# The first layer's SSM tables, rotations and rotary embedding moved from GpSimd to VectorE

## The chip, the cores and the metric

One core of a Trainium2 chip runs the kernel. The metric is the device time in microseconds, the median of several runs of the same program. The profile is of one further execution. Below, PE is the matrix engine, DVE is VectorE, ACT is ScalarE, POOL is GpSimd, and SP is the engine that issues most of the DMAs.

## The reference

Two layers of a hybrid backbone work on 512 latent tokens and 256 context tokens of width 1024. A layer norms and modulates its input (adaLN), projects it once, splits the projection into five parts, mixes tokens in three ways, projects back, and ends with a SwiGLU FFN. Cut to what the change touches:

```python
h  = modulate(rmsnorm(x, g_pre_mix), sh1, sc1) @ w_in          # the same for the context
u, f, q, k, v = jnp.split(h, splits, axis=-1)                  # 384, 256, 384, 384, 384 channels

lam_bar = jnp.exp(lam * dt)                                    # 24 groups, 64 complex states each, 2 directions
b_bar = ((lam_bar - 1) / lam)[..., None] * bmat
hc = ssm_scan(lam_bar, einsum('gph,blgh->blgp', b_bar, ucg), None, rev)
h  = ssm_scan(lam_bar, einsum('gph,blgh->blgp', b_bar, ug), h0, rev)
y  = y + einsum('ghp,blgp->blgh', cmat, h).real
z  = gelu(y);  y_ssm = z * sigmoid(z @ w_glu)

q, k = axial_rope(q, row, col), axial_rope(k, row, col)        # x1*cos - x2*sin, x2*cos + x1*sin
y_na = na_latent(q, k, v, kc, vc, na_rpb)                      # 2-D neighbourhood attention plus context
```

All inputs are 32-bit floats. The first layer also puts the context through everything; the last one leaves out the context's output.

## The kernel before

Activations lie with channels on the partitions. For each large product the left and the right side are split into a high part that PE can read (fp32r) and a low rest, and three products are added: high by high, high by low, low by high. A split is an ACT copy to the high part and a subtraction on DVE or POOL (`split`, `sub`, L579, L561). Weights come by DMA into a ring of two raw tiles and are split the same way (`wload`).

`build` (L1262) begins with the modulation vectors (`mod`), the norms of six token tiles, the scalars and powers of the SSM's eigenvalues (`scalars`, `powers`), and `make_h`: it transposes each normed tile on PE, scales and shifts it (L555, DVE), and splits it. The subtraction of the split goes to DVE for even k and to POOL for odd k.

The SSM works on chunks of 8 tokens, 96 chunk columns with the context at both ends. Twelve steps k = 2u + d go over six groups of four heads (u) and two directions (d). For each k three things are made and used:

- The tables (`prep_dir`, L430): the B table bm by three DVE operations (L447 to L449), transposed on PE (L464); the C table cl by three POOL operations of 128x576 (L452 to L456); a kernel of short lags kp on PE (L480) from cl and a padded slice b0 of bm; and the phases (`phase`, L395): index times turn, reduced to a fraction by two DVE operations, then Abs and two Sin on ACT. In the first layer they are made on the spot, one k ahead (AHEAD0); for the second they are made during the first layer's FFN, kept in DRAM and loaded again.
- The scan (`ssm_scan`, L711): PE makes the drive (L721), DVE rotates it by the phases (L725 to L728; two of the operations cross the halves of the partitions) and scans it (L731), and POOL rotates it back (L734 to L744).
- The output (`ssm_out`, L747): PE adds the states and the short lags (L756, L758); for odd k a gelu follows on ACT and DVE.

`w_in` projects eleven chunks of 128 channels: u first, then k and q in turn, then f. Chunks of q and k go through `rope` (L686): an ACT copy, a shuffle on DVE, a product on POOL (L695), a product and a sum on DVE, and splits that are stored to DRAM.

The SSM's steps are woven with the chunks of `w_in` (L1321), then come `w_v`, the Fourier mixer, the GLU and attention. The order on each engine is the framework's: a scheduler with a timeline model takes the instructions in the program's order of priority and fixes each engine's queue. In a queue the engine works in order, and an instruction that waits holds up those behind it.

Of the kernel before, what the change touches and what calls it, by code (L numbers as in the profile page):

```python
# [8 lines left out]
F32 = mybir.dt.float32  # L9
F32R = mybir.dt.float32r  # L10
I32 = mybir.dt.int32
AF = mybir.ActivationFunctionType
ALU = mybir.AluOpType
# [8 lines left out]
NH, HD = 6, 64  # L22
# [12 lines left out]
class Builder:  # L35
    def __init__(self, tc, ctx, ap):
        self.tc, self.nc, self.ap = tc, tc.nc, ap
        pool = lambda name, bufs, **k: ctx.enter_context(tc.tile_pool(name=name, bufs=bufs, **k))
        self.ring_raw = pool("ring_raw", 2)
        self.ring_hi = pool("ring_hi", 4)  # L40
        self.ring_lo = pool("ring_lo", 4)
        self.tab_p = pool("tab", 3)
        self.x_p = pool("xp", 3)
        self.g_p = pool("gp", 2)
        self.u_p = pool("up", 1)
        self.s_p = pool("sp", 24)
        self.q_p = pool("qp", 12)
        self.c_p = pool("cp", 22)
        self.z_p = pool("zp", 2)
        self.sm_p = pool("sm", 18)  # L50
        self.ss_p = pool("ss", 12)
        self.am_p = pool("am", 24)
        self.b0_p = pool("b0p", 2)
        self.keep = pool("keep", 1)
        self.ps_p = {t: pool("ps_" + t, n, space=PSUM) for t, n in (("m", 3), ("a", 2), ("t", 2), ("o", 1))}
        self.dr_p = pool("dr", 1, space=DRAM)
# [39 lines left out]
    def consts(self):  # L96
        nc = self.nc
        self.cols = self.k("cols", [128, 8])
        nc.sync.dma_start(self.cols, self.ap["cols"])
        self.ident = self.k("ident", [128, 128])  # L100
        self.nidx = self.k("nidx", [128, 96])
        self.eye16 = self.k("eye16", [128, 16])
        self.junk = self.k("junk", [128, 512], mybir.dt.bfloat16)
        self.zero = self.k("zero", [1, 128], mybir.dt.bfloat16)
        nc.vector.memset(self.zero, 0.0)
        self.sgn, self.nsgn, self.sgn2pi, self.halfpi = (self.cols[:, i:i + 1] for i in range(4))
        self.mhalf = self.cols[:, 4:5]
        self.qd = [self.dram(f"qd{l}", [NH * HD, 2, NT]) for l in range(DEPTH)]
        self.kd = [self.dram(f"kd{l}", [NH * HD, 2, NT]) for l in range(DEPTH)]
        self.ud = [self.dram(f"ud{l}", [G, HC, 8, 128]) for l in range(DEPTH)]  # L110
        self.zd = [self.dram(f"zd{l}", [G, HC, 8, 96]) for l in range(DEPTH)]
        self.tabd = [self.dram(f"tabd{l}", [NU, 2, 128, 1792]) for l in range(DEPTH)]
        self.wd = [self.dram(f"wd{l}", [NU, 128, 240]) for l in range(DEPTH)]
        self.gd = [self.dram(f"gd{l}", [4, DM]) for l in range(DEPTH)]
        self.rbd = [self.dram(f"rbd{l}", [NH, 16, 8, 384]) for l in range(DEPTH)]
        self.xd = [self.dram(f"xd{l}", [6, 128, DM]) for l in range(3)]
        self.turn = [self.k(f"turn{l}", [128, 48]) for l in range(DEPTH)]
        self.rho = [self.k(f"rho{l}", [128, 48]) for l in range(DEPTH)]
        self.mcol = [[self.k(f"mc{l}{a}", [128, 2, 16]) for a in range(3)] for l in range(DEPTH)]
        self.gcol = [self.k(f"gcol{l}", [128, 2, 8]) for l in range(DEPTH)]  # L120
        self.amod = [[self.k(f"am{l}{i}", [128, 2, 8]) for i in range(2)] for l in range(DEPTH)]
        self.dcol = [self.k(f"dcol{l}", [128, NU]) for l in range(DEPTH)]

    def consts_load(self):
        nc = self.nc
        nc.sync.dma_start(self.ident, self.ap["ident"])
        nc.sync.dma_start(self.nidx, self.ap["nidx"])
        nc.sync.dma_start(self.eye16, self.ap["eye16"])
        for l in range(DEPTH):
            nc.sync.dma_start(self.gcol[l], self.ap["gpre"][l])  # L130
            nc.sync.dma_start(self.dcol[l], self.ap["ssm_d"][l])
# [263 lines left out]
    def phase(self, l, u, d, dst):  # L395

        o = (u * 2 + d) * 4
        sh = [128, 4, 96]
        cs, sn = (dst[:, i:i + 384].rearrange("p (g n) -> p g n", g=4) for i in (0, 384))
        self.tt(sn, self.nidx.unsqueeze(1).to_broadcast(sh), self.turn[l][:, o:o + 4].unsqueeze(2).to_broadcast(sh),  # L400
                ALU.mult)
        self.ts(cs, sn, 12582912.0, ALU.add)
        self.stt(sn, cs, -12582912.0, sn, ALU.add, ALU.subtract)
        self.nc.scalar.activation(cs, sn, AF.Abs)
        self.nc.scalar.activation(cs, cs, AF.Sin, scale=-TWO_PI, bias=self.halfpi)
        self.nc.scalar.activation(sn, sn, AF.Sin, scale=self.sgn2pi)
# [23 lines left out]
    def prep_dir(self, l, fin, k, jit, tags):  # L430

        nc = self.nc
        u, d = k // 2, k % 2
        if d == 0:
            self.prep_load(l, u)
        bc, w = self.bc, self.w
        o = k * 4
        v = lambda i: bc[:, i, d * 64:(d + 1) * 64].rearrange("p (g h) -> p g h", g=4)
# [7 lines left out]
        bm, bt = xb[:, 0], xb[:, 1]  # L446
# [1 line left out]
        self.tt(bt, v(1).unsqueeze(2).to_broadcast(sb), bli.unsqueeze(3).to_broadcast(sb), ALU.mult)  # L448
        self.tt(bm, bm, bt, ALU.add)  # L449
        cl, ct = (w_.rearrange("p (g e h) -> p g e h", g=4, e=9) for w_ in (fin[:, 1632:2208], fin[:, 2208:2784]))  # L450
        g = nc.gpsimd
        g.tensor_tensor(out=cl, in0=v(2).unsqueeze(2).to_broadcast(sc), in1=clr.unsqueeze(3).to_broadcast(sc),  # L452
                        op=ALU.mult)
        g.tensor_tensor(out=ct, in0=v(3).unsqueeze(2).to_broadcast(sc), in1=cli.unsqueeze(3).to_broadcast(sc),
# [1 line left out]
        g.tensor_tensor(out=cl, in0=cl, in1=ct, op=ALU.add)  # L456
        e0 = 1 if d == 0 else 0
        clv = cl[:, :, e0:e0 + 8, :].rearrange("p g e h -> p g (e h)")
        b0 = self.b0_p.tile([128, 4, 32], F32, tag="b0", name="b0")
        nc.vector.memset(b0, 0.0)  # L460
        nc.vector.tensor_copy(b0[:, :, 0:16], bm[:, :, 0 if d == 0 else 7, :])
        tp = self.ps(tags[0], [128, 4, 128])
        for i in range(4):
            nc.tensor.transpose(tp[:, i, :], bm[:, i].rearrange("p e h -> p (e h)"), self.ident)  # L464
# [15 lines left out]
            nc.tensor.matmul(kp[32 * i:32 * i + 32, :], b0[:, i, :],  # L480
                             cl[:, i, 1 - e0:9 - e0, :].rearrange("p e h -> p (e h)"), start=True, stop=True)
        if d == 0:
            nc.vector.tensor_copy(w[:, 112:240], kp)
            self.stt(w[:, 112:128], self.eye16, self.dcol[l][:, u:u + 1], w[:, 112:128], ALU.mult, ALU.add)
        else:
            nc.vector.tensor_copy(w[:, 0:112], kp[:, 0:112])
            self.tt(w[:, 112:128], w[:, 112:128], kp[:, 112:128], ALU.add)
            nc.sync.dma_start(self.wd[l][u], w)
            if jit:
                res.append(self.toeplitz(l, u))  # L490
# [47 lines left out]
    def make_h(self, l, i, xn, t0, ks=range(8)):  # L538

        nc = self.nc  # L540
        v = 0 if t0 < 4 else 1
        if t0 in (0, 4) and ks[0] == 0:
            if t0 == 0:
                self.hh, self.hl = [[None, None] for _ in range(8)], [[None, None] for _ in range(8)]
            new = self.s if t0 == 0 else self.c
            for k in range(8):
                self.hh[k][v], self.hl[k][v] = new(F32R), new(F32R)
        cs = slice(t0 % 4 * 128, t0 % 4 * 128 + 256)
        for k in ks:
            tp = self.ps("t", [128, 2, 128])  # L550
            for j in range(2):
                nc.tensor.transpose(tp[:, j, :], xn[j][k // 4][:, k % 4 * 128:(k % 4 + 1) * 128], self.ident)  # L552
            a, s = self.amod[l][i][:, v, k:k + 1], self.modB(l, i, v, k)
            f = self.c()
            self.ts(f, tp.rearrange("p j c -> p (j c)"), a, ALU.mult, s, ALU.add)  # L555
            ins = self.split(self.hh[k][v][:, cs], self.hl[k][v][:, cs], f, nc.gpsimd if k % 2 else nc.vector)
            if t0 == 0:
                self.h_ins = ins

# [118 lines left out]
        self.fh[j], self.fl[j] = self.split2(eo, pc)  # L678

    def ev_q(self, l, j, pl, pc):  # L680
        self.rope(lambda i: self.qd[l][128 * j:128 * j + 128, i], pl, pc, -HD ** -0.5)

    def ev_k(self, l, j, pl, pc):
        self.rope(lambda i: self.kd[l][128 * j:128 * j + 128, i], pl, pc, 1.0)

    def rope(self, dst, pl, pc, scale):  # L686
        nc = self.nc
        if self.rc is None:
            self.rc, self.rs = self.s(), self.s()
# [2 lines left out]
        q, sh = self.s(), self.s()  # L692
        nc.scalar.activation(q, pl, AF.Copy, scale=scale)
        nc.vector.stream_shuffle(sh, q, [(i + 16) % 32 for i in range(32)])
        nc.gpsimd.tensor_tensor(out=sh, in0=sh, in1=self.rs, op=ALU.mult)  # L695
        self.tt(q, q, self.rc, ALU.mult)
        self.tt(q, q, sh, ALU.add)
        parts = [(q, 0, NL)]
# [12 lines left out]
    def ssm_scan(self, l, k, tab):  # L711
# [17 lines left out]
        for i in range(4):  # L729
            j = k * 4 + i  # L730
            nc.vector.tensor_tensor_scan(gg[:, i, :], self.rho[l][:, j:j + 1].to_broadcast([128, 96]),  # L731
                                         t1[:, i, :], 0.0, op0=ALU.mult, op1=ALU.add)
        gp = nc.gpsimd
        gp.tensor_tensor(out=t1, in0=gg, in1=co, op=ALU.mult)  # L734
        gp.tensor_tensor(out=t2[0:64], in0=gg[64:128], in1=si[64:128], op=ALU.mult)
        gp.tensor_tensor(out=t2[64:128], in0=gg[0:64], in1=si[0:64], op=ALU.mult)
# [10 lines left out]
    def ssm_out(self, l, k, tab, hh):  # L747
# [14 lines left out]
            self.z = self.z_p.tile([128, 8, 96], F32, tag="z", name="z")  # L762
        z = self.z
        w3 = self.q(shape=(128, 4, 96))
        nc.scalar.activation(w3, yp, AF.Square)
        self.ts(w3, w3, 0.044715, ALU.mult, 1.0, ALU.add)
        self.tt(w3, w3, yp, ALU.mult)
        nc.scalar.activation(w3, w3, AF.Tanh, scale=0.7978845608028654)
        o = (u % 2) * 4
        self.stt(z[:, o:o + 4, :], w3, 1.0, yp, ALU.add, ALU.mult)  # L770
# [679 lines left out]
```

## Time and profile before

| | us |
|---|---|
| median of 3 runs | 1678.88 (1678.62 to 1682.22) |
| profiled execution | 1677.44 |
| its span, first to last instruction | 1675.6 |
| PE busy in the span | 1596.9 |
| DVE busy | 1037.3 |
| ACT busy | 608.9 |
| POOL busy | 378.8 |

The span is what the profile shows of the 1677.44 us. Busy time of an engine is the time in which at least one of its instructions runs; an engine runs its instructions in order, and the next one may start a little before the end of the last. [...]

### The profile page before, as it was taken

The numbers are of one execution on the slowest core, as the hardware profiler recorded it, in microseconds if no ns is written. First come the engines' busy times: TensorE is split into PE (matmuls) and PEld (weight loads), VectorE is DVE, ScalarE is ACT, GpSimd is POOL, SyncE is SP. The second block draws the span as 40 slices with busy tenths as digits, with TensorE's granted clock in tenths as the row PEclk, the third lists the DMA queues.
The fourth block names the chain that finished last, engine by engine and source line by source line (L and its number), as shares of the span: only waits on it lengthen the run. The fifth ranks groups of instructions, "written<-read, shape, count | busy, mean of one in ns | idle before, by whom it ended". The sixth has DMA issues, their size and how long they took to land. (4 is left out here: it accounts for less than half of the span.)

```text
span 1675.6 us, 23600 instructions
## 1 busy us (share of the span) xinstructions
PE 1596.9 (95%) x9097; PEld 1311.2 (78%) x9097; DVE 1037.3 (62%) x1911; ACT 608.9 (36%) x1101; POOL 378.8 (23%) x384
## 2 busy tenths in 40 slices
PE   5988789999999999999999999999999999999997
PEld 1777676678898788878787788988778888888886
DVE  7799985774774667434434348698773634455455
ACT  5434344654627322112211127321563532222222
POOL 3367773100310323100000005276410100000002
PEclk8999799999999999999999999999899999999999
DMA  9343339662313334534423537367713322233222
GB/s 327 128 136 111 100 101 306 225 217 94 127 57 138 129 119 142 195 114 163 148 105 114 191 114 236 132 233 227 228 52 139 139 101 101 76 102 102 97 78 85
DMA packets 101391, 240.08 MB, mean 143 GB/s; under 512 B 25424, under 2 KB 56784, under 8 KB 88480
## 3 DMA queue, kind: packets, MB, share of 16 engines
q1 hardware_dynamic: 97968, 229.93, 40.3%
q0 software_dynamic: 3312, 8.65, 1.7%
q8 instruction: 71, 1.16, 0.3%
q14 instruction: 40, 0.33, 0.1%
HBM read 201.26 MB, written 38.47 MB: 143 GB/s over the span
## 5 line engine op out<-in xcount | busy, mean ns | idle before, releaser
L589 PE MATMUL b<-s,wh 128*128 128x512 f32 (+1 forms) x1856 | 553.6, 377 | 2.3 <-ACT s L580 0.8
L589 PEld LDWEIGHTS b<-s,wh 128*128 128x128 f32 x1856 | 339.9, 190 | 73.9 <-issue 10.6
L589 PE MATMUL b<-s,wl 128*128 128x512 f32 (+1 forms) x928 | 346.8, 375 | 2.5 <-DVE wl L561 2.5
L580 ACT ACTIVATE wh<-wr 128x1024 fp32r<-128x1024 f32 (+4 forms) x184 | 185.0, 1026 | 337.8 <-PE b L589 240.3
L561 DVE TENSOR_TENSOR wl<-wr,wh 128x1024 fp32r<-128x1024 f32 (+4 forms) x184 | 224.5, 1236 | 101.9 <-ACT wh L580 96.6
L278 DVE TENSOR_TENSOR q<-q,b 128x512 f32<-128x512 f32 (+1 forms) x192 | 129.2, 675 | 166.0 <-PE b L1178 165.3
L589 PEld LDWEIGHTS b<-s,wl 128*128 128x128 f32 x928 | 176.0, 190 | 33.2 <-DVE wl L561 3.8
L589 PE MATMUL b<-c,wh 128*128 128x256 f32 x944 | 183.8, 289 | 0.0
L589 PEld LDWEIGHTS b<-c,wh 128*128 128x128 f32 x944 | 154.7, 195 | 5.9 <-issue 0.6
L281 DVE SCALAR_TENSOR_TENSOR s<-s,b 128x512 f32<-128x512 f32 x88 | 60.2, 684 | 132.8 <-PE b L589 84.3
L1178 PE MATMUL b<-wh,tab 128*128 128x512 f32 x400 | 137.2, 393 | 0.1
L589 PE MATMUL b<-c,wl 128*128 128x256 f32 x472 | 134.9, 288 | 0.0
L1178 PE MATMUL b<-wh,s 128*128 128x512 f32 x384 | 129.5, 391 | 0.0
L1210 POOL TENSOR_TENSOR q<-q,g 128x512 f32<-128x512 f32 x10 | 13.8, 1380 | 361.2 <-ACT junk L515 335.5
L589 PEld LDWEIGHTS b<-c,wl 128*128 128x128 f32 x472 | 92.5, 196 | 1.7 <-issue 0.4
L1178 PEld LDWEIGHTS b<-wh,tab 128*128 128x128 f32 x400 | 75.1, 188 | 19.4 <-ACT c L1155 2.5
L1178 PEld LDWEIGHTS b<-wh,s 128*128 128x128 f32 x384 | 72.1, 188 | 19.9 <-ACT c L1155 2.5
L1178 PE MATMUL b<-wl,tab 128*128 128x512 f32 x200 | 78.3, 392 | 0.0
L1178 PE MATMUL b<-wl,s 128*128 128x512 f32 x192 | 74.6, 390 | 0.0
L527 POOL TENSOR_TENSOR ss<-ss,cols 128x1 f32<-128x1 f32 x42 | 31.0, 739 | 192.2 <-DVE ss L281 191.5
L580 ACT ACTIVATE s<-s 128x512 fp32r<-128x512 f32 x43 | 27.0, 627 | 122.0 <-DVE s L281 58.5
L452 POOL TENSOR_TENSOR u<-x,u 128x576 f32<-128x576 f32 x24 | 30.7, 1280 | 175.2 <-PE b L480 142.7
(311 smaller groups left out, 2735.8 us busy)
## 6 DMA issues: line engine op xcount, KB each, us to landing
wr<-in_w_gu SPq DMA_DIRECT2D x44, 1024.0 KB
wmod<-in_w_mod SPq DMA_DIRECT2D x46, 512.0 KB
wr<-in_w_down SPq DMA_DIRECT2D x22, 1024.0 KB
wmod<-in_w_mod SPq DMA_DIRECT2D x16, 1024.0 KB
wr<-in_w_in SPq DMA_DIRECT2D x10, 1024.0 KB
u<-in_w_mod SPq DMA_DIRECT2D x18, 512.0 KB
wr<-in_w_out SPq DMA_DIRECT2D x8, 1024.0 KB
tab<-tabd SPq DMA_DIRECT2D x12, 640.0 KB
```

The lines of the kernel that those rows point to most:

```text
L278: self.nc.vector.tensor_tensor(out=out, in0=a, in1=b, op=op)
L281: self.nc.vector.scalar_tensor_tensor(out=out, in0=a, scalar=s, in1=b, op0=op0, op1=op1)
L452: g.tensor_tensor(out=cl, in0=v(2).unsqueeze(2).to_broadcast(sc), in1=clr.unsqueeze(3).to_broadcast(sc), op=ALU.mult)
L527: nc.gpsimd.tensor_tensor(out=ss[:, 3:4], in0=ss[:, 2:3], in1=self.mhalf, op=ALU.pow)
L561: (eng or self.nc.vector).tensor_tensor(out=lo, in0=x, in1=hi.bitcast(F32), op=ALU.subtract)
L580: ins = self.nc.scalar.activation(hi, x, AF.Copy)
L589: self.nc.tensor.matmul(out, a[k], h[k][v][:, cs], start=(k == 0 and i == 0), stop=(k == 7 and i == 2))
L1178: nc.tensor.matmul(pd, a[v][:, cs], w[:, ds], start=(j == 0 and i == 0), stop=(j == n - 1 and i == 2))
L1210: (nc.gpsimd, nc.vector)[hf].tensor_tensor(out=oo[hf], in0=oo[hf], in1=gates[t // 4][:, hf * 512:(hf + 1) * 512], op=ALU.mult)
```

## The change

In the first layer (where the tables are made on the spot, `jit`) the three operations of the C table, the rotation back after the scan and rope's product run on DVE instead of POOL. So does the subtraction of the split in the first `make_h`. The second layer keeps these on POOL. In both layers the product of index and turn in `phase` becomes four ACT activations with a scale per partition, one for each of the four heads (`phases`, which makes the second layer's, is left as it is); the copies into b0 and out of kp go to ACT; b0 becomes two kept tiles that POOL zeroes once at the start, instead of a memset on DVE each time; `make_h` scales and shifts on ACT for odd k; and the gelu's factor moves into the square, so that one DVE operation less is left.

```diff
     def consts_load(self):
         nc.sync.dma_start(self.ident, self.ap["ident"])
+        for b0 in self.b0:
+            nc.gpsimd.memset(b0, 0.0)
...
     def phase(self, l, u, d, dst):
-        self.tt(sn, self.nidx.unsqueeze(1).to_broadcast(sh), self.turn[l][:, o:o + 4].unsqueeze(2).to_broadcast(sh),
-                ALU.mult)
+        for g in range(4):
+            self.nc.scalar.activation(sn[:, g, :], self.nidx, AF.Identity, scale=self.turn[l][:, o + g:o + g + 1])
...
     def prep_dir(...):
-        g = nc.gpsimd
+        g = nc.vector if jit else nc.gpsimd
...
-        b0 = self.b0_p.tile([128, 4, 32], F32, tag="b0", name="b0")
-        nc.vector.memset(b0, 0.0)
-        nc.vector.tensor_copy(b0[:, :, 0:16], bm[:, :, 0 if d == 0 else 7, :])
+        b0 = self.b0[k % 2]
+        nc.scalar.activation(b0[:, :, 0:16], bm[:, :, 0 if d == 0 else 7, :], AF.Copy)
...
-            nc.vector.tensor_copy(w[:, 112:240], kp)
+            nc.scalar.activation(w[:, 112:240], kp, AF.Copy)
...
-            nc.vector.tensor_copy(w[:, 0:112], kp[:, 0:112])
+            nc.scalar.activation(w[:, 0:112], kp[:, 0:112], AF.Copy)
...
     def make_h(...):
-            self.ts(f, tp.rearrange("p j c -> p (j c)"), a, ALU.mult, s, ALU.add)
-            ins = self.split(self.hh[k][v][:, cs], self.hl[k][v][:, cs], f, nc.gpsimd if k % 2 else nc.vector)
+            if k % 2:
+                nc.scalar.activation(f, tp.rearrange("p j c -> p (j c)"), AF.Identity, scale=a, bias=s)
+            else:
+                self.ts(f, tp.rearrange("p j c -> p (j c)"), a, ALU.mult, s, ALU.add)
+            ins = self.split(self.hh[k][v][:, cs], self.hl[k][v][:, cs], f,
+                             nc.gpsimd if k % 2 and (l, i) != (0, 0) else nc.vector)
...
     def rope(self, l, dst, pl, pc, scale):
-        nc.gpsimd.tensor_tensor(out=sh, in0=sh, in1=self.rs, op=ALU.mult)
+        (nc.vector if l == 0 else nc.gpsimd).tensor_tensor(out=sh, in0=sh, in1=self.rs, op=ALU.mult)
...
     def ssm_scan(...):
-        gp = nc.gpsimd
+        gp = nc.vector if l == 0 else nc.gpsimd
...
     def ssm_out(...):
-        nc.scalar.activation(w3, yp, AF.Square)
-        self.ts(w3, w3, 0.044715, ALU.mult, 1.0, ALU.add)
-        self.tt(w3, w3, yp, ALU.mult)
+        nc.scalar.activation(w3, yp, AF.Square, scale=0.044715 ** 0.5)
+        self.stt(w3, w3, 1.0, yp, ALU.add, ALU.mult)
```

## Rows read from the trace of the kernel before

**Rows 1.** Busy time by stretches: start:end, length, engines (instructions), PE clock, DMA share, GB/s

```profile
36.00:54.00 18.00, 13.12 (x65) 6.29 (x65) 15.38 (x25) 7.44 (x16) 10.75 (x8) 0.91 0.70 256
97.00:241.00 144.00, 115.11 (x709) 99.48 (x708) 143.28 (x240) 55.96 (x102) 108.06 (x87) 0.88 0.32 100
412.00:445.00 33.00, 30.87 (x199) 27.59 (x198) 27.19 (x63) 25.37 (x56) 12.46 (x15) 1.00 0.51 175
```

**Rows 2.** Waits of PE, 97 to 252 us: total, times, longest

```profile
PE b L480 <- POOL u L456: 12.4, 3, 6.8
PE b L464 <- DVE x L278: 11.1, 4, 3.1
```

**Rows 3.** DVE groups by shape, 97 to 241 us: busy, mean ns, idle before

```profile
L278 DVE TENSOR_TENSOR x<-x,u 128x512 f32<-128x512 f32 x20 | 21.0, 1079 | 0.1
L278 DVE TENSOR_TENSOR q<-q 128x384 f32<-128x384 f32 x11 | 11.5, 1044 | 0.0
...
L278 DVE TENSOR_TENSOR q<-b,tab 64x384 f32<-64x384 f32 x20 | 11.1, 555 | 0.3
L278 DVE TENSOR_TENSOR tab<-nidx,turn 128x384 f32<-128x384 f32 x9 | 10.4, 1150 | 0.0
...
L278 DVE TENSOR_TENSOR x<-x 128x512 f32<-128x512 f32 x10 | 10.1, 1006 | 0.0
L281 DVE SCALAR_TENSOR_TENSOR tab<-tab 128x384 f32<-128x384 f32 x10 | 8.3, 827 | 0.1
L561 DVE TENSOR_TENSOR s<-s 128x512 fp32r<-128x512 f32 x7 | 7.6, 1093 | 0.0
L275 DVE TENSOR_SCALAR tab<-tab 128x384 f32<-128x384 f32 x10 | 7.2, 720 | 0.0
L461 DVE COPY b<-x 128x64 f32<-128x64 f32 x10 | 6.9, 691 | 0.0
L561 DVE TENSOR_TENSOR c<-c 128x256 fp32r<-128x256 f32 x6 | 6.8, 1140 | 0.0
...
L275 DVE TENSOR_SCALAR q<-q 128x384 f32<-128x384 f32 x4 | 3.8, 951 | 0.0
```

**Rows 4.** Timeline, 85 to 135 us: start, length, engine, instruction

```profile
85.25 1.28 DVE L278 TENSOR_TENSOR x<-x,u 128x512 f32<-128x512 f32 x2
...
91.37 1.69 DVE L278 TENSOR_TENSOR q<-b,tab 128x384 f32<-128x384 f32 x3
...
94.23 0.55 DVE L278 TENSOR_TENSOR tab<-nidx,turn 128x384 f32<-128x384 f32 x1
...
95.11 0.63 DVE L561 TENSOR_TENSOR s<-s 128x512 fp32r<-128x512 f32 x1
...
130.50 4.34 POOL L734 TENSOR_TENSOR q<-q,tab 128x384 f32<-128x384 f32 x1 [2.71 <-DVE q L731]
...
131.46 0.34 DVE L275 TENSOR_SCALAR tab<-tab 128x384 f32<-128x384 f32 x1
...
131.73 0.41 DVE L561 TENSOR_TENSOR c<-c 128x256 fp32r<-128x256 f32 x1
...
134.81 0.55 DVE L281 SCALAR_TENSOR_TENSOR tab<-tab 128x384 f32<-128x384 f32 x1
```

**Rows 5.** POOL groups by shape, 97 to 260 us

```profile
L736 POOL TENSOR_TENSOR q<-q,tab 64x384 f32<-64x384 f32 x12 | 14.7, 1222 | 0.7
L452 POOL TENSOR_TENSOR u<-x,u 128x576 f32<-128x576 f32 x10 | 13.9, 1395 | 7.7 <-ACT q L470 7.4
```

**Rows 6.** ACT groups by shape, 97 to 241 us

```profile
L580 ACT ACTIVATE c<-c 128x256 fp32r<-128x256 f32 x5 | 2.0, 409 | 0.1
```

**Rows 7.** Waits of ACT, 97 to 241 us

```profile
ACT tab L404 <- DVE tab L281: 33.8, 9, 8.6
```

**Rows 8.** Waits of PE, 0 to 60 us

```profile
PE b L552 <- DVE c L275: 6.1, 2, 3.8
```

**Rows 9.** Waits of DVE, 1080 to 1200 us (second layer's SSM stage)

```profile
DVE q L275 <- ACT q L765: 5.6, 3, 3.5
```

More of the change, by code (lines that the diff above doesn't have):

```diff
@@ L52, in __init__ @@
         self.am_p = pool("am", 24)
-        self.b0_p = pool("b0p", 2)
         self.keep = pool("keep", 1)
@@ L101, in consts @@
         self.nidx = self.k("nidx", [128, 96])
+        self.b0 = [self.k(f"b0{i}", [128, 4, 32]) for i in range(2)]
         self.eye16 = self.k("eye16", [128, 16])
@@ L397, in phase @@
         o = (u * 2 + d) * 4
-        sh = [128, 4, 96]
         cs, sn = (dst[:, i:i + 384].rearrange("p (g n) -> p g n", g=4) for i in (0, 384))
-        self.tt(sn, self.nidx.unsqueeze(1).to_broadcast(sh), self.turn[l][:, o:o + 4].unsqueeze(2).to_broadcast(sh),
-                ALU.mult)
+        for g in range(4):
+            self.nc.scalar.activation(sn[:, g, :], self.nidx, AF.Identity, scale=self.turn[l][:, o + g:o + g + 1])
         self.ts(cs, sn, 12582912.0, ALU.add)
@@ L680, in ev_q, with rope @@
     def ev_q(self, l, j, pl, pc):
-        self.rope(lambda i: self.qd[l][128 * j:128 * j + 128, i], pl, pc, -HD ** -0.5)
+        self.rope(l, lambda i: self.qd[l][128 * j:128 * j + 128, i], pl, pc, -HD ** -0.5)
     def ev_k(self, l, j, pl, pc):
-        self.rope(lambda i: self.kd[l][128 * j:128 * j + 128, i], pl, pc, 1.0)
-    def rope(self, dst, pl, pc, scale):
+        self.rope(l, lambda i: self.kd[l][128 * j:128 * j + 128, i], pl, pc, 1.0)
+    def rope(self, l, dst, pl, pc, scale):
         nc = self.nc
```

## The prediction

> **What bounds the kernel now.** I read the busy time by stretches first. Outside the first 60 us, the layer boundaries and the two SSM stages PE is busy all the time, so what can move is where it is not. The largest such place is the first layer's SSM stage: from 97 to 241 us PE is busy 115.1 of 144 us at a granted clock of 0.88 (so part of it at the lower of the two levels), DVE 143.3, ACT 56.0 and POOL 108.1 [rows 1]. The reader is to see that DVE has no free time there, and that POOL has three quarters of its time filled with the work that the change takes from it. The waits of PE in this stage are for tables: 12.4 us before L480 for the C table from POOL, 11.1 us before L464 for the B table from DVE [rows 2]. Both tables come from engines that share the stage, so the next question is what sets DVE's 143 us.
>
> For that I read DVE's groups in the stage, shapes apart [rows 3], against the same forms at moments when POOL had nothing to do or stood still [rows 4]. An operation with two SBUF inputs takes far longer in the stage: 128x512 1079 ns, where two quiet ones together take 1.28 us (0.69 each, less an overlap); 128x384 1044 ns against 0.55. A 64x384 one that reads its first input from PSUM takes 555 ns in the stage, and three such operations in a row 1.69 us at a quiet moment, which is no difference. Copies and tensor_scalar from SBUF suffer as well: 691 ns for a 128x64 copy, 720 for the 128x384 tensor_scalar that takes 0.34 when it is alone. At 131 us the same is seen from the other side: DVE runs five such operations at their short price, and the POOL product beside them lasts 4.34 us, where the mean of its half-width kin is 1.22 [rows 4, 5]. I read this as DVE and POOL taking turns at SBUF, one standing while the other runs; what reads PSUM is spared.
>
> **The change, part by part, in the stage 97 to 241 us.** Times are sums of single durations; the overlap comes at the end.
>
> (a) POOL goes quiet, so DVE's forms fall to their quiet price [rows 3, 4]: x<-x,u 20 x (1.08 - 0.69) = 7.8 us; the like 128x512 products and sums x<-x and s<-s, 20 of about 1.01, 6.4; q<-q 11 x (1.04 - 0.55) = 5.4; the stt of the phases 10 x (0.83 - 0.55) = 2.8; its tensor_scalar 10 x (0.72 - 0.34) = 3.8; the s splits 7 x (1.09 - 0.63) = 3.2; the c splits 6 x (1.14 - 0.41) = 4.4. That is 33.8. Weight splits and the diagonal's stt, of the same kind, add about 2. Together -35.8.
>
> (b) What leaves DVE [rows 3]: the phase product 9 x 1.15 = 10.4; the copy into b0 10 x 0.69 = 6.9; nine copies of kp and nine memsets of b0, 0.15 to 0.3 each and not shown, 3.9; the tensor_scalar of the gelu, folded into an stt, 4 x 0.95 = 3.8. Together -25.0.
>
> (c) What comes to DVE. POOL's records give the counts: the three C-table operations of 128x576 29 times (10, 9 and 10 for its three lines), the rotations 12 + 12 + 12, their subtractions [rows 5]. No 128x576 operation stands on DVE in the trace. From 0.55 (384) and 0.69 (512) the slope is 1.1 ns per column, so 0.76; bounded from below by the 0.69 of 512 columns, from above by the hindered price, 1.08 x 576/512 = 1.21. I take 0.76, the nearest quiet row: 22.0 us. Rotations 36 x 0.55 = 19.8 (the two that cross the halves of the partitions move the same 384 columns). Subtractions: six of 380 columns at 0.55, six of 256 and of 124 at 0.41 and 0.27: 7.4. Memsets of one column, 12 of about 0.1: 1.2. Rope's product 5 x 0.69 = 3.5. Together +53.9.
>
> (d) Overlap. DVE's 235 records in the stage last 160 us in sum and fill 143.3, so each starts about 0.07 us ahead of the end of the one in front. The three operations q<-b,tab that cross the halves do not: 0.54 + 0.55 + 0.55 make 1.69 [rows 4]. There are 59 records more after the change. I give no overlap to the 36 that cross the halves or come right behind one: 23 x 0.07 = -1.6.
>
> Sum: -35.8 - 25.0 + 53.9 - 1.6 = -8.5 us of 144. So a stage that gets 54 us of work comes out a little shorter. DVE still bounds it (135 us of DVE, 115 of PE), and a full PE follows, so the 8.5 us go to the end time. If all 36 overlapped it would be -11. [...]
>
> Beside these ACT gets, in the stage, 38 products of 96 columns, 10 copies into b0 and 9 of kp. A 128x256 activation takes 0.41 [rows 6], so these take at most 0.41 each, 23 us at the most, more likely some 15. ACT has 56 of 144, so the work itself hides behind DVE. The two memsets that POOL gets at the start cost nothing (POOL is idle there), no DMA is added, and nothing of POOL's is waited for in this layer until attention.
>
> **The start.** The first make_h loses its POOL splits and half its tensor_scalars go to ACT. From 36 to 54 us DVE is busy 15.4 of 18 [rows 1], and PE waits 6.1 us for the modulated h from DVE [rows 8]. There DVE's hindered forms give back about 4.0 us, half the tensor_scalars 1.2, the phase product and b0 0.7; four splits (0.36 after overlap) and three C products bring 1.4 and 2.1: net -2.4. I take -2; the bounds are 0 and the 6.1 us of waiting.
>
> **Layer 1 and the boundaries.** The folded gelu spares layer 1's SSM stage six tensor_scalars of 0.6 us; DVE waits 5.6 us in front of them for ACT's square [rows 9], and that wait only moves to the stt. I take -1 (0 to -3.6). At the three later make_h passes a product of 0.54 goes from DVE to ACT for every odd k. In 412 to 445 us DVE has 27.2 and ACT 25.4 of 33 us [rows 1]; seven at 0.41 make ACT 28.3 and DVE 23.5. ACT then is the fuller one; I take +1 for all three (-3 to +5). The prep of layer 1 gets its copies on ACT in the FFN, where PE is full: 0.
>
> **Sum.** -8.5 - 2 - 1 + 1 = -10.5 us: 1677.4 for the profiled execution (span 1675.6) becomes 1666.9. The median of the runs, 1678.9, lies 1.4 above that execution; carried over, 1668.4.
>
> **Rivals.** (A) The hindrance isn't POOL's: DMA or ACT slow DVE's SBUF operations, and they stay as long. Then (a) falls away, and 65 added operations cost about 0.47 us more each (+31 us) at the worst; with (b) alone against (c) it is already +27, so 1706. For it: the stage has DMA at 0.32. Against it: the spared PSUM readers, and the 0.34 to 0.55 us that the same forms take in the stage while POOL stands still, its product stretched to 4.34 [rows 4].
> (B) The slower side: DVE waits for ACT. It has no wait in the stage now. After the change its tensor_scalar of each table needs four products from ACT, whose queue is in order and stands still behind its Abs, 33.8 us over nine waits for DVE's stt [rows 7]. If the products are queued behind such an Abs, or behind a weight split, DVE stops, and all that is queued behind it on DVE (scans, rotations, splits, and so PE). Twelve tables: from 0.9 us per table the gain is gone; at 2 us it is 24 - 10.5 = +13.5, 1692. Against it: the products need nothing but the turn table and a free buffer, so they can be early.
> (C) No change: PE runs its queue in order, and its waits for tables come from the order rather than from DVE's total; the 8.5 us are given back as DVE idle. Then only start and layer 1 count, within 3 us: 1677.
> (D) More: the start gives all 6 us, layer 1 3.6, the crossing operations overlap (-11), the boundaries gain 1: -22, 1657.
>
> **Chances.** Forecast (-4 to -17 us) 0.58, D 0.10, C 0.10, B 0.15, A 0.07. A change of 0.2%, 3.4 us, is about what can be told from none. Faster 0.68, same 0.11, slower 0.21. The range goes from 1650 (D, a little beyond) to 1690 (half of B); by itself the forecast's range is 1662 to 1675.
>
> **What would show it.** POOL nearly empty from 30 to 250 us; DVE's x<-x,u at 0.69 and q<-q at 0.55 in the stage; the C products at 0.76; DVE at 95% or more of a stage that ends some 10 us earlier; ACT near 70 us there; no wait of DVE for ACT above 1 us. Wrong if DVE's two-input forms stay near 1 us (A), if DVE shows idle time with ACT as its releaser (B), or if the stage ends where it did with DVE partly idle (C).

## The result, and the profile after

The changed kernel takes 1657.7 us (median; 1653.8 to 1664.2) against 1679.7 for the kernel before on the same chip: a ratio of 0.987, with a 95% interval of 0.985 to 0.989, so 22 us faster, about twice the forecast gain of 10.5. Its profiled execution took 1655.9 us, with a span of 1654.1 (before 1675.6).

The page's first part gives the engines' busy time over the whole span:

```profile
PE 1588.4 (96%) x9097; PEld 1305.8 (79%) x9097; DVE 996.6 (60%) x1891; ACT 651.9 (39%) x1241; POOL 237.2 (14%) x266
```

PE has the same 9097 matmuls as before and 8.5 us less busy time (1596.9 before; the mean granted clock, as a share of the full one, rose from 0.977 to 0.983). It stands idle for 65.7 us of the span, where it stood for 78.7. So the 21.5 us of span are 13.0 of idle time and 8.5 of matmuls that ran less often at the lower clock: in slices of 1 us the granted clock is 0.50 in 64 of 1675 slices before and in 47 of 1654 after, and 1.00 in 1586 and 1592. POOL's busy time fell by 142 us, and DVE's, which took over much of that work, fell too, by 41.

Where the time left is best read from two lines of matmuls, those that drive the scans (b<-U,tab, 96 of them in the first layer) and those that give the SSM's output (b<-q); each row has count, mean ns (smallest/mean/largest), and first to last start. Before:

```profile
L721 PE MATMUL b<-U,tab x96: 243/275/421, 90.2 to 243.0; 128*128 128x96 f32 x96
L756 PE MATMUL b<-q x96: 243/275/350, 112.0 to 263.1; 128*128 128x96 f32 x96
```

After:

```profile
L725 PE MATMUL b<-U,tab x96: 244/275/350, 84.4 to 222.4; 128*128 128x96 f32 x96
L760 PE MATMUL b<-q x96: 243/275/422, 100.3 to 242.1; 128*128 128x96 f32 x96
```

The stage from first to last drive fell from 152.8 to 138.0 us (-14.8), and it begins 5.8 us earlier. The other 0.9 us of the 21.5 lie behind it: the last SSM output is 21.0 us earlier, the first attention score 19.7 (254.5 to 234.8), the last down projection 21.5 (1665.4 to 1643.9).

Busy time by stretches, in the columns of [rows 1]; first the drive stretch of the kernel before, as the fair partner to the second row of after:

```profile
90.20:243.00 152.80, 123.92 (x767) 106.76 (x767) 150.91 (x256) 61.13 (x111) 111.00 (x90) 0.89 0.35 108
```

After, the start, the drive stretch and a boundary ([rows 1] has their like):

```profile
36.00:54.00 18.00, 17.34 (x106) 11.04 (x105) 16.27 (x37) 11.89 (x29) 0.00 (x0) 0.96 0.79 280
84.40:222.40 138.00, 120.12 (x787) 105.89 (x786) 134.31 (x291) 77.92 (x172) 0.91 (x1) 0.94 0.40 120
391.00:425.00 34.00, 32.85 (x215) 29.73 (x214) 23.77 (x56) 28.16 (x64) 10.37 (x17) 1.00 0.56 191
```

POOL is empty (0.91 us), DVE is still full (134.3 of 138.0), with 35 instructions more in 16.6 us less. PE does 20 matmuls more in the shorter stretch, at a clock of 0.94 for 0.89.

DVE's groups by shape in this stretch (columns of [rows 3]):

```profile
L280 DVE TENSOR_TENSOR x<-x,u 128x512 f32<-128x512 f32 x20 | 13.0, 684 | 2.5 <-DMA x<-in_ssm_bc 2.4
L280 DVE TENSOR_TENSOR q<-b,tab 64x384 f32<-64x384 f32 x22 | 12.2, 555 | 0.3
...
L453 DVE TENSOR_TENSOR u<-x,u 128x576 f32<-128x576 f32 x10 | 7.6, 755 | 0.1
L738 DVE TENSOR_TENSOR q<-q,tab 128x384 f32<-128x384 f32 x10 | 5.5, 552 | 0.0
L739 DVE TENSOR_TENSOR q<-q,tab 64x384 f32<-64x384 f32 x10 | 5.5, 554 | 0.1
L280 DVE TENSOR_TENSOR q<-q 128x384 f32<-128x384 f32 x10 | 5.5, 551 | 0.1
L277 DVE TENSOR_SCALAR tab<-tab 128x384 f32<-128x384 f32 x10 | 3.5, 352 | 0.0
...
L565 DVE TENSOR_TENSOR c<-c 128x256 fp32r<-128x256 f32 x6 | 2.5, 418 | 0.0
```

Against [rows 3]: 1079 ns became 684, 1044 became 551, 720 became 352, 1140 became 418, and the form that reads PSUM stayed at 555. The added forms cost what their nearest quiet rows said: 755 for 576 columns (forecast 760), 552 for a rotation (550). The x10 of the rotations will matter below: ten sets, not twelve.

Two waits that the rivals spoke of. The only DVE wait from 85 to 225 us (total, times, longest) is for a load, none is for ACT:

```profile
DVE x L280 <- DMA x<-in_ssm_bc: 2.4, 1, 2.4
```

And of PE in the first 60 us, the wait for DVE's modulated h [rows 8] is gone, and a small one for ACT's is left:

```profile
PE b L552 <- ACT c L556: 1.7, 2, 1.0
```

### The profile page after: what moved, and what is told of

Same layout as the page of the kernel before. It is cut to its first block, busy times and chain, and to the rows that moved or that the text cites. A ratio compares the mean times of both kernels' runs of the same rounds, so it can differ in the third digit from the quotient of the medians.

```text
span 1654.1 us, 23548 instructions
## 1 busy us (share of the span) xinstructions
PE 1588.4 (96%) x9097; PEld 1305.8 (79%) x9097; DVE 996.6 (60%) x1891; ACT 651.9 (39%) x1241; POOL 237.2 (14%) x266
## 5 line engine op out<-in xcount | busy, mean ns | idle before, releaser
L565 DVE TENSOR_TENSOR wl<-wr,wh 128x1024 fp32r<-128x1024 f32 (+4 forms) x184 | 221.1, 1217 | 110.0 <-ACT wh L584 100.4
L280 DVE TENSOR_TENSOR q<-q,b 128x512 f32<-128x512 f32 x180 | 122.7, 684 | 165.6 <-PE b L1181 165.0
L593 PE MATMUL b<-c,wh 128*128 128x256 f32 x944 | 179.1, 284 | 0.0
L593 PEld LDWEIGHTS b<-c,wh 128*128 128x128 f32 x944 | 151.3, 191 | 5.5 <-issue 0.6
L593 PEld LDWEIGHTS b<-c,wl 128*128 128x128 f32 x472 | 90.2, 191 | 1.4 <-issue 0.2
L1213 POOL TENSOR_TENSOR q<-q,g 128x512 f32<-128x512 f32 x10 | 13.9, 1392 | 367.0 <-ACT junk L515 336.1
L1158 ACT ACTIVATE s<-b 128x512 f32<-128x512 f32 x44 | 25.9, 589 | 78.1 <-PE b L593 78.1
```

The source lines that it names most:

```text
L280: self.nc.vector.tensor_tensor(out=out, in0=a, in1=b, op=op)
L565: (eng or self.nc.vector).tensor_tensor(out=lo, in0=x, in1=hi.bitcast(F32), op=ALU.subtract)
L593: self.nc.tensor.matmul(out, a[k], h[k][v][:, cs], start=(k == 0 and i == 0), stop=(k == 7 and i == 2))
L1158: nc.scalar.activation(tmp[v], gp, AF.Tanh, scale=0.5)
L1213: (nc.gpsimd, nc.vector)[hf].tensor_tensor(out=oo[hf], in0=oo[hf], in1=gates[t // 4][:, hf * 512:(hf + 1) * 512], op=ALU.mult)
```

## The experiments

Each was timed beside the kernel before on its own chip; the ratios are to that. The changed kernel's own is 0.987.

**Is it the neighbour? POOL given work again.** The changed kernel, with three POOL products per scan call in the first layer that nobody reads (36 in all):

```diff
         gp = nc.vector if l == 0 else nc.gpsimd
+        if l == 0:
+            for _ in range(3):
+                nc.gpsimd.tensor_tensor(out=self.junk[:, 0:384].rearrange("p (g c) -> p g c", g=4), in0=co, in1=si, op=ALU.mult)
```

> Changed kernel with three more POOL products of 128x384 per SSM step of layer 0 (36, about 1.02 us each when alone, 37 us), that read the phase table and write where nobody reads in that stage. Nothing waits for their result. Taking turns: DVE's two-input forms rise above their quiet price again, what reads PSUM stays at 0.55, and by the ratio of before (48 us of DVE for 108 us of POOL) the stage gets some 16 us longer: 1674. Rival, DVE's long durations had another cause: x<-x,u stays at 0.69 and the time at 1658.

Measured: 0.9968 [0.9956, 0.9980], 1675.8 us, some 17 us of the 22 gone; the last SSM output moves from 242.1 to 260.9. Its stretch (the extra products are the 36.12 us of the fifth column), three hindered DVE forms and the spared one:

```profile
85.00:238.00 153.00, 125.50 (x790) 110.23 (x789) 151.40 (x291) 77.95 (x173) 36.12 (x30) 0.91 0.35 108
```

```profile
L280 DVE TENSOR_TENSOR x<-x,u 128x512 f32<-128x512 f32 x20 | 15.0, 786 | 0.5 <-DMA x<-in_ssm_bc 0.4
...
L280 DVE TENSOR_TENSOR x<-x 128x512 f32<-128x512 f32 x11 | 11.1, 1008 | 0.1
L455 DVE TENSOR_TENSOR u<-x,u 128x576 f32<-128x576 f32 x10 | 9.1, 909 | 0.0
L280 DVE TENSOR_TENSOR q<-b,tab 64x384 f32<-64x384 f32 x22 | 12.2, 554 | 0.3
```

DVE has the same 291 instructions and needs 151.4 us for them instead of 134.3: 36 us of useless work beside it cost it 17 us, on its SBUF forms alone. Rival A, that DMA or ACT slow those forms, falls by this: DMA's share is lower here (0.35 for 0.40), ACT's work the same (77.95 us for 77.92). Of the forms with all inputs in SBUF x<-x,u goes from 684 to 786 ns, x<-x from 688 to 1008 and the phases' tensor_scalar from 352 to 432 in the same trace, while q<-q stays at 551; the one that reads PSUM takes 554 for 555. DVE has no copy left in this stretch.

**The moves alone.** The kernel before, with only POOL's work put on DVE:

```diff
-        g = nc.gpsimd
+        g = nc.vector if jit else nc.gpsimd
...
-        nc.gpsimd.tensor_tensor(out=sh, in0=sh, in1=self.rs, op=ALU.mult)
+        (nc.vector if l == 0 else nc.gpsimd).tensor_tensor(out=sh, in0=sh, in1=self.rs, op=ALU.mult)
...
-        gp = nc.gpsimd
+        gp = nc.vector if l == 0 else nc.gpsimd
```

> Kernel before with only the moves from POOL to DVE in layer 0 (C table, rotations back, rope's product); phase product, b0, kp, gelu and make_h as before. Taking turns (DVE and POOL hinder each other at SBUF): DVE in the stage pays the moved work at 0.55 to 0.76 us each and gets its hindrance back, but keeps some 9.5 us (quiet price) that the changed kernel gives to ACT; the stage ends 4 to 5 us earlier, the time falls by about 5 us to 1675. Rival, the hindrance is not POOL's and ACT's part of the change makes the gain: the moved 50 us come on top, 1700 or more, and x<-x,u stays near 1.08 us.

Measured: 1.0003 [0.9991, 1.0015], no change at all. The stage gave more than was expected of it: drives from 87.8 to 230.0 (142.2 us, for 152.8, where 4 to 5 us were expected), last SSM output 5.2 us earlier, first score 7.9 earlier. But the time is given back right there: the last score is 1.3 us later than before. Stretches of this kernel at the junction to attention, and ACT's wait in it, in front of a copy of w_v's results into va, for the store of the lag kernel w (wd<-x):

```profile
240.00:245.00 5.00, 2.42 (x19) 1.05 (x9) 1.57 (x4) 1.25 (x3) 0.99 (x2) 0.90 1.06 369
...
255.00:260.00 5.00, 3.39 (x25) 1.98 (x23) 0.95 (x3) 0.49 (x2) 1.12 (x2) 1.00 0.95 363
260.00:265.00 5.00, 4.37 (x20) 2.56 (x20) 4.36 (x15) 3.66 (x9) 1.89 (x3) 0.61 0.53 156
265.00:270.00 5.00, 5.00 (x23) 4.01 (x20) 2.00 (x6) 0.71 (x3) 0.73 (x1) 0.50 0.48 102
270.00:275.00 5.00, 5.00 (x29) 2.35 (x28) 1.51 (x6) 2.60 (x6) 0.72 (x1) 0.53 0.89 313
```

```profile
ACT va L638 <- DMA wd<-x: 9.5, 2, 6.0
```

PE idles for some 5 us in the first three of these rows, then runs for some 15 us at a granted clock of 0.50 to 0.61, which costs 6 to 7 more (an estimate from the last three rows: 0.39 x 4.4 + 0.50 x 5 + 0.47 x 5 if a matmul's time goes with the clock; in the trace before three matmuls of b<-c take 0.36 us at 1.00 and 0.64 at 0.50). From first to last score the attention takes 98.3 us, where it took 88.9 before and 88.1 after.

**What leaves DVE, alone.** The kernel before, with the phase products, the copies into b0 and of kp on ACT, the kept b0 and the folded gelu (these lines of the diff, nothing else).

> Kernel before with only what goes from DVE to ACT inside the SSM (phase product, b0 copy, kp copies, gelu factor) and the kept b0; POOL keeps its work. Taking turns: the operations taken off DVE are worth their quiet price, some 9.5 us in the stage, since the time they stood waiting for POOL is then stood by others: 1670. Rival, hindered durations are the operations' own cost: 25 us of records less 3 of overlap leave DVE, 1658, and the whole gain of the change would be this part.

Measured: 0.9983 [0.9972, 0.9995], 2 to 3 us. Both expectations were too hopeful: 25 us of instructions leave a DVE that bounds the stage, and the time does not follow. The stretch between its drives, and two of its groups on DVE:

```profile
91.00:238.00 147.00, 120.83 (x750) 105.21 (x748) 136.76 (x207) 76.24 (x171) 102.75 (x87) 0.90 0.38 113
```

```profile
L280 DVE TENSOR_TENSOR x<-x,u 128x512 f32<-128x512 f32 x20 | 27.2, 1392 | 8.1 <-DMA x<-in_ssm_bc 4.8 <-DMA wd<-x 3.2
L731 DVE TENSOR_TENSOR_SCAN q<-rho,q 128x96 f32<-128x96 f32 x41 | 17.3, 478 | 0.1
```

The scans in the kernel before, 97 to 241 us:

```profile
L731 DVE TENSOR_TENSOR_SCAN q<-rho,q 128x96 f32<-128x96 f32 x41 | 11.3, 330 | 0.0
```

Between the drives 26.4 us of DVE's records are gone, but its busy time falls by 14.1 us only (150.9 to 136.8). The large products rise from 1079 [rows 3] to 1392 ns and the scans from 330 to 478, 20 x 0.31 + 41 x 0.15 = 12 us; other forms fall (the c splits from 1140 to 550 ns, q<-q from 1044 to 762). Over all forms that stand in both stretches some 10 us more go to the same work, beside a POOL that is about as busy as before (70% of the stretch, for 73%). DVE also idles 10.2 us instead of 1.9, 8.1 of them in front of x<-x,u for two DMAs, as the row shows. So the stretch is shorter by 5.9 us, and behind it that is lost: POOL's rotations come late (they wait 38 us in all for the scans), and the last SSM output is at 269.3, 6 us later than before.

**The edits of make_h, alone and left out.** make_h_only is the kernel before with them; no_make_h is the changed kernel without them:

```diff
-            if k % 2:
-                nc.scalar.activation(f, tp.rearrange("p j c -> p (j c)"), AF.Identity, scale=a, bias=s)
-            else:
-                self.ts(f, tp.rearrange("p j c -> p (j c)"), a, ALU.mult, s, ALU.add)
-            ins = self.split(self.hh[k][v][:, cs], self.hl[k][v][:, cs], f,
-                             nc.gpsimd if k % 2 and (l, i) != (0, 0) else nc.vector)
+            self.ts(f, tp.rearrange("p j c -> p (j c)"), a, ALU.mult, s, ALU.add)
+            ins = self.split(self.hh[k][v][:, cs], self.hl[k][v][:, cs], f, nc.gpsimd if k % 2 else nc.vector)
```

> Kernel before with only make_h changed (odd k scaled on ACT everywhere, splits of the first make_h on DVE). If the start gives what the two traces show (the first SSM drive 5.8 us earlier), the time falls by 4 to 6 us, 1674 to 1676. Rival, as the prediction had it: 2 us, 1678; in that case the rest of the earlier start comes from POOL's C table being off SBUF.

> Changed kernel with make_h as before. If the start term is 5 to 6 us and adds to the stage: 1663. If it is 2 us: 1660. If DVE's stage takes up the later start: 1658, no loss.

Measured: alone 1.0009 [0.9998, 1.0020]; left out 0.9884 [0.9859, 0.9910], which can't be told from the whole change. Without them the first drive is at 87.4 instead of 84.4, but the first score at 233.8 instead of 234.8: their 3 us at the start are lost again inside the stage. Alone they don't bring the first drive forward at all (90.9 for 90.2, in the profiled execution, the slowest of twelve). The other 2.8 us of the earlier start come from the other edits; the moves alone put the first drive at 87.8. And since no_make_h is the moves and the offload together, these two, worth nothing and 0.2% by themselves, make 1.2% as a pair.

**The ACT scaling in the first make_h alone** (the changed kernel, with `if k % 2 and (l, i) == (0, 0):` for `if k % 2:`):

> Changed kernel where odd k of make_h go to ACT only in the very first make_h; at the three later layer boundaries all are scaled on DVE as before. The prediction had +1 us for the boundaries: then 1657. If ACT is what they wait for: 1654. If the shift to ACT helped there: 1660.

Measured: 0.9850 [0.9837, 0.9864], 1655.8 us; the intervals overlap the changed kernel's. At the boundary DVE now is the fuller engine (27.6 for ACT's 25.4, where it was 23.8 and 28.2 above), and PE does 9 matmuls fewer in this stretch (206 for 215), of which the end time shows nothing:

```profile
391.00:425.00 34.00, 31.89 (x206) 28.57 (x206) 27.55 (x63) 25.36 (x56) 13.18 (x16) 1.00 0.55 180
```

**The phase product back on DVE** in the changed kernel (phase() as before):

> Changed kernel with the phase product back on DVE as one operation per table (12 x 0.55 us, 0.48 after overlap, 5.8 in all) instead of four on ACT. DVE bounds the stage: 5 to 6 us slower than the changed kernel, 1663. Rival, ACT's queue or PE's bounds it: no change, or faster by what ACT loses, 1658 or less.

Measured: 0.9918 [0.9901, 0.9936], about 8 us lost. The group is there at its quiet price:

```profile
L280 DVE TENSOR_TENSOR tab<-nidx,turn 128x384 f32<-128x384 f32 x10 | 5.5, 552 | 0.0
```

Ten products are 5.5 us, but the last drive moves by only 1.9 us, and the last SSM output by 10.5 (252.6). More is lost in the tail of the stage than the products themselves take; two waits there name the same transfer as in moves_only and a DVE that stands for ACT:

```profile
ACT va L643 <- DMA wd<-x: 9.1, 2, 6.1
DVE q L283 <- ACT q L770: 8.8, 2, 4.7
```

The first score comes only 2.0 us later than in the changed kernel, the last one 13.1. The first layer's attention, from first to last score, in the kernel before, the changed one, moves_only and this one; the last two idle a little and run at a lower clock:

```profile
254.50:343.40 88.90, 88.90 (x712) 59.41 (x713) 56.71 (x149) 49.13 (x118) 21.50 (x33) 1.00 0.79 258
234.80:322.90 88.10, 86.03 (x686) 58.09 (x686) 58.88 (x156) 49.10 (x117) 19.38 (x28) 1.00 0.78 252
246.50:344.80 98.30, 96.06 (x704) 65.05 (x703) 61.84 (x164) 52.13 (x121) 18.39 (x28) 0.93 0.74 239
236.80:336.00 99.20, 96.98 (x716) 65.95 (x718) 63.46 (x166) 53.70 (x125) 18.40 (x28) 0.95 0.75 246
```

**The same moves in the second layer** (rotations and the rope product on DVE for both layers):

> Changed kernel with the rotations back and rope's product on DVE in layer 1 as well. DVE gets about 30 us in layer 1's SSM stage and gets some 27 us of hindrance back by the ratio of layer 0; the stage has DVE at 83 of 100 us, so no change within 3 us is likeliest: 1658. If the wait of PE for POOL's rotations (2.6 us before) counts most: 1655. If DVE becomes the bound there: 1661 or more.

Measured: 0.9929 [0.9910, 0.9948], some 10 us worse than the change. The second layer's SSM stage, first in the changed kernel, then here:

```profile
1061.00:1145.00 84.00, 77.99 (x466) 69.58 (x465) 76.05 (x133) 19.96 (x39) 53.58 (x57) 0.96 0.76 235
```

```profile
1061.00:1148.00 87.00, 84.49 (x523) 77.65 (x521) 81.66 (x187) 25.20 (x47) 0.00 (x0) 1.00 0.74 230
```

DVE takes 54 instructions more for 5.6 us more busy time, 0.1 us each where a rotation takes 0.55 in the first layer, so the others take less time here too (an estimate from these counts), but DVE, at 91% of this stage before, is at 94% of a longer one. The last drive comes 3.3 us later (1148.1), the last SSM output 7.8 (1174.0), and from 1140 to 1200 us PE's granted clock is 0.74 for 0.89. That DVE had no room is the likely reason, but not shown: the planner (the framework's scheduler) also put this layer's w_v matmuls 13 us earlier (1105.7 for 1119.0).

**A buffer of its own for w.** w is the tile into which kp is copied and which is then stored to DRAM; va takes its buffers from the same pool. To take away the va wait seen in moves_only, w got a buffer of another pool in the first layer, in three kernels:

```diff
+        if l == 0:
+            self.w = self.c(shape=(128, 240))
```

> The moves alone (as moves_only) with the lag kernel w in a buffer of its own in layer 0, so that the copies of w_v's results on ACT need not wait for w's store. In moves_only ACT stood 6.0 us before such a copy at the end of the SSM, with the last gelu behind it, and the last SSM output came 27.9 us after the last drive, against 19.7 in the changed kernel. If that wait gives back the gain of the moves: last output 6 to 8 us earlier, 1672 to 1675. Rival, the order that the planner finds or PE's clock gives it back: no change, 1680.

> Phase product back on DVE (as product_on_dve) with w in its own buffer in layer 0. product_on_dve lost 8 us where its DVE work is worth 5.8, and has the same 6.1 us wait of ACT at the end. If the wait makes the surplus: 2 to 4 us faster than product_on_dve, 1663 to 1665. If all of the 8 us hangs on it: 1659. Rival: no change, 1667.

> Changed kernel with w in its own buffer in layer 0. Its ACT waits only 0.5 us at that place, so no change is expected: 1657 to 1658. If it gets slower, the buffer itself (one of the context tiles' pool) costs something, which the two others then carry too.

Measured: 1.0024 [1.0014, 1.0035] on the moves alone, 0.9931 [0.9919, 0.9943] on product_on_dve, 0.9913 [0.9899, 0.9927] on the changed kernel. No gain anywhere, and in the last a loss of 7 us. The wait for the store is gone in all three (in front of va ACT now waits for PE's matmuls, 12.6 to 14.1 us), but the edit did more than that: the planner put the attention's w_v matmuls late in all three, at 226.5, 218.6 and 217.3 us, where without it they begin at 177.0, 176.3 and 172.0. So these runs don't test the wait by itself. From first to last score the attention takes 93.7, 88.5 and 88.7 us in them, for 98.3, 99.2 and 88.1: the loss at the junction is smaller or gone where the wait is gone, but the first score now comes 11.9 to 14.1 us later. In the last of them the last drive came 11 us earlier (211.4), with w_v behind it. The same stretch in the changed kernel and in this one:

```profile
85.00:220.00 135.00, 117.12 (x763) 103.32 (x763) 131.41 (x286) 75.37 (x168) 0.91 (x1) 0.94 0.40 120
```

```profile
85.00:220.00 135.00, 111.90 (x675) 95.19 (x675) 133.10 (x290) 76.14 (x169) 1.48 (x2) 0.86 0.37 112
```

PE did 88 matmuls fewer while DVE was the bound, at a lower clock, and had them to do afterwards: first score at 247.9 instead of 234.8.

**A little more off DVE.** after_own_w with the boundary edit above, and with the rounding step of the phases done by ACT too (magic is a column that holds 12582912):

```diff
-        self.ts(cs, sn, 12582912.0, ALU.add)
+            self.nc.scalar.activation(cs[:, g, :], self.nidx, AF.Identity, scale=self.turn[l][:, o + g:o + g + 1],
+                                      bias=self.magic)
```

> Changed kernel with w in its own buffer, ACT's scaling of odd k only in the first make_h, and the phases' rounding step on ACT too (four more activations of 96 columns per table, with a bias, instead of DVE's tensor_scalar). If DVE bounds the stage: ten times 0.28 us less, 3 us faster, 1653 to 1655. Rival, ACT (78 of 138 us) gets so full that DVE waits for it: 1660 or more.

Measured: 0.9906 [0.9891, 0.9920]; the last drive comes 3.4 us before after_own_w's (208.0), so DVE bounds the drives there as well, but at the end the two can't be told apart (1663.0 for 1664.2 us). No kernel tried is told to be faster than the changed one.

## Why the prediction was right in kind and too small by half

**The mechanism held**, as far as durations show it: x<-x,u takes 1079 ns beside POOL's 108 us of work, 684 with POOL empty and 786 beside 36 us of useless products, and the form that reads PSUM 554 to 555 in all three. That the two engines take turns at SBUF, one standing while the other runs, is the prediction's reading of such durations; no trace shows the standing itself. The quiet prices were right within some 4% (but for the s splits, 681 ns for 630, and the memsets), DVE stays the bound and a stage with some 48 us of new work comes out shorter. Part (a), forecast at -35.8 us, measured -34.9 from the mean durations of both traces. ACT came to 77.9 us in the stage rather than near 70 (16.8 more than in the same stretch before, for "more likely some 15"), and hid them all.

**Term (c) was mis-sized.** "Rotations 36 x 0.55", "the rotations 12 + 12 + 12" of [rows 5]: that view reached to 260 us, where the terms (a) and (b) were counted to 241. From 97 to 241 us POOL has ten sets in the trace before, too. In the changed kernel ten sets fall before the last drive, the last two into the tail, where PE has other work. With the subtractions and memsets that go with them, (c) is 47.9 us, not 53.9. The rest between first and last drive: (b) -26.4 for -25.0 (a tenth phase product), one group of scans fewer -1.1, other changes of count next to nothing, overlap -2.1 for -1.6. Sum -34.9 - 26.4 + 47.9 - 1.1 - 2.1 = -16.6 us of DVE time (150.9 to 134.3), of which -14.8 shows as stage, since DVE idles 1.8 us more. Forecast: -8.5; of the 8.1 us between, 6.0 are (c).

**The start was undersized, and partly for a wrong reason.** "I take -2" against 5.8 us at the first drive, close to the bound of 6.1. The forecast took it from DVE's work between 36 and 54 us, the first make_h above all; but no_make_h shows that make_h's 3 us of it are not worth anything at the end, and alone these edits give no earlier start. So the stage's own 14.8 and the start's 5.8 aren't two separate gains: with an earlier start the stage takes longer (138.0 us, and 133.8 in no_make_h, for the same end).

**That the stage's gain reached the end was partly luck.** That "a full PE follows, so the 8.5 us go to the end time" held for the change. The same step fails in moves_only, where 12.9 us at the last drive are all given back behind it, and in product_on_dve, where 1.9 us there become 13.1 at the last score. Nothing in the prediction told these cases apart.

**Layer 1 (the second layer) and the boundaries** were forecast at -1 and +1. Behind the first layer's last output only 0.5 us were gained; from the second layer's first drive to its first score there are 110.2 us before and 110.8 after, so the folded gelu gave nothing that can be seen. The ACT scaling at the boundaries can't be told from zero (act_scale_first_only).

**The rivals.** B didn't happen: from 85 to 225 us DVE has no wait for ACT, and ACT's wait behind its Abs fell from 33.8 [rows 7] to 15.3 us. A is refuted by pool_beside. C, that a shorter DVE gains nothing, is wrong for this change, but not absurd: in moves_only a stage shorter by 10.6 us gained nothing, and after_own_w, with its drives done 11 us earlier, lost 7. D named the right time by the wrong terms, which is luck: the start gave nearly its 6 us, but layer 1 and the boundaries gave nothing, and the crossing operations don't overlap. In the trace after, an ordinary pair, and a rotation that crosses the halves behind another (start, duration):

```profile
119.84 0.56 DVE L280 TENSOR_TENSOR q<-q 128x384 f32<-128x384 f32 x1
120.31 0.69 DVE L699 TENSOR_TENSOR s<-s 128x512 f32<-128x512 f32 x1
...
127.91 0.55 DVE L739 TENSOR_TENSOR q<-q,tab 64x384 f32<-64x384 f32 x1
128.48 0.55 DVE L740 TENSOR_TENSOR q<-q,tab 64x384 f32<-64x384 f32 x1
```

The crossing one starts 0.57 us behind the other's start, after its end; the ordinary one 0.47 us behind, 0.09 before the other's end. In the twelve sets of rotations in the first layer of this trace the crossing ones start 0.55 to 0.58 us behind the operation in front, which lasts 0.54 to 0.56.

**What was not foreseen at all** is that the two halves need each other. The offload without the moves leaves DVE beside POOL's work (x<-x,u at 1392 ns), the moves without the offload lose at the junction what they gain in the stage. Shown is that the loss lies there (late va, 5 us of idle PE, then a granted clock of 0.50 to 0.61). What triggers it stays open: the attention takes 98.3 and 99.2 us in the two kernels with the long va wait and 93.7 and 88.5 in the same two without it, but the edit that took the wait away also moved w_v. Open as well is how much of the 22 us is owed to the order: w_v begins at 172.0 in the changed kernel and at 209.7 before, but at 177.0 in moves_only too, which gained nothing.

## What to carry to other kernels

Busy time of DVE beside a busy POOL was here partly hindrance (1079 ns for an x<-x,u of 684): price each operation at its quiet duration, add what the neighbour gives back, and don't count an operation removed beside a neighbour that stays as time won (offload_only). A shorter stage is not yet a shorter kernel: look at where its gain could be given back (moves_only). Count every term of a stage's sum over the same window, and ask of the engine that takes the work whether it has room (the first layer had, by what POOL gave back; the second, with DVE at 91%, likely had not). Where a planner orders the work, look after each edit for what it now puts into the stage's gaps: here another buffer for one tile moved a group of matmuls by 45 us and cost 7.

## What the runs showed of the hardware beyond that

The hindrance isn't a fixed price: with less for DVE to do, the same product beside the same POOL work went from 1079 to 1392 ns and the scan from 330 to 478, while the c splits fell from 1140 to 550; over all forms it was 10 us more. Memsets of 128x4 take 62 ns on DVE, where 100 was the estimate, and a 64x384 product that reads PSUM takes 554 to 555 ns in the first layer's stage of six kernels (before, after, moves_only, offload_only, pool_beside, product_on_dve), with POOL busy for 103 to 111 us of the stage, for 36 or for 1.
